# A two-layer trunk on one core: pacing of the modulation's row tiles beside the output projection, and another buffer pool for two filter tables

## The chip, the core and the metric

The kernel runs on one core of a Trainium2 chip. The metric is the device time of one execution in microseconds. Five engines take part: TensorE (PE) for matmuls, VectorE (DVE), ScalarE (ACT), GpSimd (POOL, nearly unused here) and SyncE (SP), whose queue issues nearly all loads. Each engine takes its instructions in one fixed order and waits at the first one that is not ready.

## The reference

A trunk of two layers over 256 tokens of width 2048, with 256 context tokens beside them. Each sub-layer is an RMS norm, modulated by shift, scale and gate vectors that are linear in the conditioning vector, then a mixer, then a gated residual.

```python
def _rms(x, g):
    xf = x.astype(jnp.float32)
    y = xf * lax.rsqrt(jnp.mean(xf * xf, axis=-1, keepdims=True) + EPS)
    return (y * g.astype(jnp.float32)).astype(x.dtype)
```

Layer 0 mixes with attention, layer 1 with an order-2 Hyena: projections, short convolutions, and long convolutions with filters that a small sine network makes from positions and that a decay table multiplies. Both layers end with a ConvGLU channel mixer of width 5632. The modulation has six vectors (parts 0 to 5) a layer: part (l, j) is the product of the conditioning vector with a 2048 x 2048 block of a weight matrix, plus a bias.

## The kernel before

All matmuls are in fp32 by parts: each operand is split into a high and a low part, and three products are summed (`products`, L343; `mm3`, L347 to L349). Weights come in blocks of 512 KB by SP (`wload`, L328) into a ring of six buffers ("raw"). `wsplit` makes the high part on ACT (L334) and the low part on DVE (L335), into rings of three each ("whi", "wlo").

The modulation's first two parts of layer 0 are made at the start on PE (`ada_block`, L924, its result copied by ACT into `adast`), from 512 KB loads that borrow the rings raw, whi, wlo and "araw" (six buffers, NAR). The other ten parts are made row tile by row tile on DVE: the class `Ada` has 32 row tiles for a part; `one()` issues the load of one tile into "araw" (L476) and, four tiles behind (LAG), multiplies and sums one tile in a single DVE instruction (L486, called a row sum below). L490 and L491 close a part. `drive(gen, rate, ada_rate)` runs a stage and, at each of its yields, adds `ada_rate` to a credit, of which each whole one pays for one `one()`. `need((l, j))` makes at once what a part still lacks. The flag `calm[0]` sets the rate to nothing:

```python
            ada_bg.step(0.0 if calm[0] else ada_rate if not isinstance(ada_rate, tuple) else ada_rate[0] if up else ada_rate[1])
```

`proj_out`, the output projection of every sub-layer, sets it for each of its steps, the last one true:

```python
                    calm[0] = final and half == 1 and i == n - 1
```

Only `proj_out` and the up projection of the channel mixer set it, so the Hyena's projections and convolutions (HY_ADA) run with what layer 0's channel mixer left. The Hyena's own output projection runs with HO_ADA:

```python
    drive(proj_out(hw_out, OUT_PASSES, h2split, adaV[:, 1, 2], xs, accs), HO_RATE, HO_ADA)
    need((1, 3), (1, 4))
```

Behind it stands the norm of layer 1's channel mixer: sums of squares on PE (L382), a reciprocal root by Newton steps of a few small DVE instructions (L384, L364 to L374, L390), and a broadcast on PE (L391). The channel mixer's first matmuls wait for that.

At the start `filters(DCS[0], True)` makes the spectra of the first two of four column blocks of the Hyena filters. For each block it loads the network's last weights (`w3`, L629, two halves of 256 KB) and the decay table (`dec`, L630, 512 KB), splits w3 on ACT and DVE (`w3s`, L358, L359), multiplies on PE (L347 to L349) and scales by the decay table (`hf`, L590). The start also takes the squares and norms of x and of the context (L662, L666, L671). Pool "q4" has 24 buffers of 512 KB, in which most tiles of the start and of the later stages live.

Of the kernel before, what the change touches and what calls it, by code (L numbers as in the profile page):

```python
# [12 lines left out]
F32 = mybir.dt.float32  # L13
# [6 lines left out]
P = 128  # L20
# [162 lines left out]
START_RATE = 2.0, 1.4  # L183
Q_RATE = 6.5
O_RATE = 5.2
KV_ADA, Q_ADA, O_ADA, HY_ADA, HO_ADA = 1.9, 0.7, 0.8, 0.2, 0.2
F0_ADA, F1_ADA = (0.7, 0.6), (0.4, 0.2)
EV_RATE, FLY, LAG = 1.0, 8, 4
DCS = (0, 1), (2,), (3,)
# [6 lines left out]
def trunk_kernel(ctx, tc, out, xT, cT, cols, rows, f_w0, f_w12, f_w3, ada_w, ada_t, w_in, w_out, hw_in, hw_out,  # L196
# [3 lines left out]
    NQ4, NS2, NRAW, NW, NAR = 24, 11, 6, 3, 6  # L200

    pool = ctx.enter_context(tc.tile_pool(name="pool", bufs=1))
# [4 lines left out]
    def nm(s):  # L207
        uid[0] += 1
        return f"{s}{uid[0]}"

    def q4(shape, dt=F32, name="q"):
        return pool.tile(shape, dt, tag="q4", bufs=NQ4, name=nm(name))

    def s2(shape, dt=F32, name="s"):
        return pool.tile(shape, dt, tag="s2", bufs=NS2, name=nm(name))
# [130 lines left out]
    def mm3(o, lh, ll, rh, rl, first, last, **kw):  # L346
        PE.matmul(o, lh, rh, start=first, stop=False, **kw)  # L347
        PE.matmul(o, lh, rl, start=False, stop=False, **kw)  # L348
        PE.matmul(o, ll, rh, start=False, stop=last, **kw)  # L349
# [7 lines left out]
    def split(hi, lo, src):  # L357
        A.copy(hi, src)  # L358
        V.tensor_tensor(lo, src, hi, op=ALU.subtract)  # L359
# [157 lines left out]
    def split_const(off, n, name, out=None):  # L517
        hi, lo = out or (q4([P, n], F32R, name + x) for x in "hl")
        for h in range(n // 512):
            t = s2([P, 512], F32, "fgt")  # L520
            c = slice(512 * h, 512 * h + 512)
            SP.dma_start(t, k_fg[:, off + 512 * h: off + 512 * h + 512])
            split(hi[:, c], lo[:, c], t)
        return hi, lo
# [40 lines left out]
    def filters(dcs, spare=False):  # L565

        if not dcs:
            return
        fhl = q4([P, 1024], F32R, "fm")
        split_const(0, 512, "f", (fhl[:, 0:512], fhl[:, 512:1024]))  # L570
        fh, fl = (fhl[:, i * 512:(i + 1) * 512].rearrange("p (t f) -> p t f", t=2) for i in range(2))
        w3v = f_w3.rearrange("w (o d c) -> w o d c", o=2, d=2)

        late = []

        def finish():
            for dst, sums in late:
                V.reciprocal(dst, sums)
            late.clear()

        def samples(o, dc, w3, dec, hl):
            nn = []
            for tt in range(2):
                ab = []
                for i, (sh, sl_) in enumerate(layers):
                    p = ftag[0]()
                    t = slice(tt * P, (tt + 1) * P)
                    mm3(p, sh[:, t], sl_[:, t], w3[0][:, o], w3[1][:, o], True, True)
                    h = s2([P, 512], F32, "hf")
                    V.tensor_tensor(h, p, dec[:, tt], op=ALU.mult)  # L590
                    split(hl[2 * i][:, tt], hl[2 * i + 1][:, tt], h)
                    A.activation(h, h, AF.Abs)
                    ab.append(h)
                    finish()
                    yield

                V.tensor_tensor(ab[0], ab[0], ab[1], op=ALU.max)
                nn.append(ab[0])
            V.tensor_tensor(nn[0], nn[0], nn[1], op=ALU.add)
            pn = ftag[0]()  # L600
            for c in range(4):
                PE.matmul(pn[:, c:c + 1], nn[0][:, c * P:(c + 1) * P], ones[:, 0:1], start=True, stop=True)
            late.append((invn[:, o, dc * 4:dc * 4 + 4], pn[:, 0:4]))

        def spectra(o, dc, hl):
            for half in range(2):
                so = q4([P, 2, 512], F32, "spo")
                xh, xl = hl[2 * half], hl[2 * half + 1]
                c = slice(half * P, (half + 1) * P)
                pe, po = ftag[0](), ftag[0]()  # L610
                mm3(pe, fh[:, 0, c], fl[:, 0, c], xh[:, 0], xl[:, 0], True, True)
                mm3(po, fh[:, 1, c], fl[:, 1, c], xh[:, 1], xl[:, 1], True, True)
                e = s2([P, 512], F32, "se")
                A.activation(e, pe, AF.Copy, scale=1.0 / (2 * T))
                V.scalar_tensor_tensor(out=so[:, 0], in0=po, scalar=1.0 / (2 * T), in1=e, op0=ALU.mult, op1=ALU.add)
                V.scalar_tensor_tensor(out=so[:, 1], in0=po, scalar=(half * 2 - 1) / (2 * T), in1=e, op0=ALU.mult,
                                       op1=ALU.subtract if half else ALU.add)
                yield
                A.dma_start(spec[o][dc][:, 2 * half:2 * half + 2], so)

        before = []
        for dc in dcs:
            if spare:
                w3 = pool.tile([P, 2, 512], F32, tag="araw", bufs=NAR, name=nm("w3"))
                dec = pool.tile([P, 2, 512], F32, tag="araw", bufs=NAR, name=nm("dec"))
            else:
                w3, dec = (q4([P, 2, 512], F32, "w3") for _ in range(2))
            for d in range(2):
                SP.dma_start(w3[d * HW:(d + 1) * HW], w3v[:, :, d, dc * 512:(dc + 1) * 512])  # L629
            SP.dma_start(dec, k_decay[:, :, dc * 512:(dc + 1) * 512])  # L630
            w3s = [q4([P, 2, 512], F32R, "w3s") for _ in range(2)]
            split(*w3s, w3)
            yield
            for o in range(2):
                hl = [q4([P, 2, 512], F32R, "fhl") for _ in range(4)]
                yield from samples(o, dc, w3s, dec, hl)
                if spare and before:
                    yield from spectra(*before.pop())
                before.append((o, dc, hl))
        if not spare:  # L640
            fill_rate[0] = 0.0
        finish()
        for b in before:
            yield from spectra(*b)
# [292 lines left out]

    bg.add(filter_net(), "filters")
    bg.add(filters(DCS[0], True), "filters")
    norm_bg = Bg()  # L940
    xg, cg = [], []
# [200 lines left out]
    def fill(dcs, at, rate):  # L1142

        def hook(*now):
            ftag[0] = HI4 if now[0] == 0 else LO4
            if dcs and now == at:
                fill_bg.add(filters(dcs), "fill")
                fill_bg.one()
                fill_rate[0] = rate
        return hook  # L1150
# [201 lines left out]
```

## Time and profile before

| what | value |
|---|---|
| median of 3 runs | 2630.94 us (2628.95 to 2631.34) |
| the profiled execution | 2630.88 us, its span 2629.1 us |
| granted PE clock, mean | 0.979 |
| PE busy | 2527.7 us (96%) |
| weight loads of PE busy | 2347.2 us (89%) |
| DVE busy | 1965.5 us (75%) |
| ACT busy | 1258.8 us (48%) |
| row sums L486 on DVE | 320, together 387.6 us |

Times of places are microseconds from the span's start. PE is close to always busy, so time is to be had or lost where PE waits: in the first 180 us, and at the seams between sub-layers.

### The profile page before, as it was taken

The page shows a single profiled execution, that of the slowest core. Times are in us where ns is not written, and L with a number is a line of the kernel's source. Part 1 is how long each engine was busy: PE and PEld are TensorE (multiplying, and loading weights), DVE is VectorE, ACT ScalarE, POOL GpSimd, SP SyncE. Part 2 cuts the span into 40 slices and gives each one's busy share as a digit, 9 for nine tenths or more (in the row PEclk, how much of TensorE's full clock was granted, in tenths as well). Part 3 has the DMA queues.
Part 4 walks back from the last instruction along what each step waited for, and adds up shares of the span by engine and source line. Part 5 has one row for each costly group of instructions (what it writes and reads, how often), then busy time and mean ns, then how long its engine had stood idle before and what let it go on. Part 6 is the DMA issues. An engine that isn't in the chain of part 4 may idle for free.

```text
span 2629.1 us, 48048 instructions
## 1 busy us (share of the span) xinstructions
PE 2527.7 (96%) x19502; PEld 2347.2 (89%) x19502; DVE 1965.5 (75%) x3071; ACT 1258.8 (48%) x1801; POOL 0.7 (0%) x6
## 2 busy tenths in 40 slices
PE   5889999999799999999999999999799999999999
PEld 2558886678799999999998999998799999999999
DVE  6637858877888888888878788889776755556664
ACT  3352235664544444445545655554354444445543
POOL 0000000000000000000000000000000000000000
PEclk7899999999899999999999999999899999999999
DMA  7777876557599999998897565555678766666664
GB/s 276 274 307 248 273 254 216 156 173 252 174 331 322 331 327 330 329 328 309 288 343 261 175 194 174 182 178 200 232 256 268 255 193 194 196 194 193 193 208 138
DMA packets 176726, 639.19 MB, mean 243 GB/s; under 512 B 19735, under 2 KB 19832, under 8 KB 176504
## 3 DMA queue, kind: packets, MB, share of 16 engines
q1 hardware_dynamic: 174200, 627.74, 71.8%
q10 hardware_dynamic: 2304, 8.39, 0.8%
q8 instruction: 152, 2.49, 0.4%
q14 instruction: 70, 0.57, 0.1%
HBM read 623.47 MB, written 12.58 MB: 242 GB/s over the span
## 4 chain that ended last, share of the span: by engine, by line
PE 90%; DVE 6%; ACT 3%; DMA 1%; issue 1%; SPq 0%; ACTq 0%; DVEq 0%
PE ps_proj L343 23%; PE ps_hy L343 9%; PE ps_kv L343 7%; PE ps_q L343 3%; PE ps_ada L343 2%; PE ps_ada L924 1%; PE ps_attn L853 1%; PE ps_attn L814 1%; DVE wlo_proj L335 1%; DVE araw_ada L486 1%; ACT whi_proj L334 1%; PE ps_conv L347 1%; PE ps_conv L348 1%; PE ps_conv L349 0%; PE ps_attn L773 0%
## 5 line engine op out<-in xcount | busy, mean ns | idle before, releaser
L335 DVE TENSOR_TENSOR wlo_proj<-raw_proj,whi_proj 128x1024 fp32r<-128x1024 f32 x240 | 292.4, 1222 | 144.2 <-ACT whi_proj L334 143.0
L334 ACT CAST whi_proj<-raw_proj 128x1024 fp32r<-128x1024 f32 x240 | 251.9, 1054 | 292.1 <-PE ps_proj L343 260.8
L486 DVE SCALAR_TENSOR_TENSOR araw_ada<-araw_ada,slB 128x1024 f32<-128x1024 f32 x320 | 387.6, 1218 | 0.0
L343 PE MATMUL ps_proj<-ph,whi_proj 128*128 128x256 f32 x1408 | 192.6, 277 | 1.1 <-ACT ph L358 1.0
L343 PE MATMUL ps_proj<-pl,whi_proj 128*128 128x256 f32 x1408 | 191.7, 277 | 0.0
L343 PE MATMUL ps_proj<-ph,wlo_proj 128*128 128x256 f32 x1408 | 191.1, 276 | 0.0
L343 PEld LDWEIGHTS ps_proj<-ph,whi_proj 128*128 128x128 f32 x1408 | 174.5, 188 | 2.8 <-ACT ph L358 1.7
L343 PEld LDWEIGHTS ps_proj<-pl,whi_proj 128*128 128x128 f32 x1408 | 174.4, 188 | 0.4 <-DVE pl L359 0.3
L343 PEld LDWEIGHTS ps_proj<-ph,wlo_proj 128*128 128x128 f32 x1408 | 174.1, 188 | 0.0
L334 ACT CAST whi_hy<-raw_hy 128x1024 fp32r<-128x1024 f32 x96 | 101.3, 1056 | 106.4 <-PE ps_hy L343 77.5
L335 DVE TENSOR_TENSOR wlo_hy<-raw_hy,whi_hy 128x1024 fp32r<-128x1024 f32 x96 | 116.3, 1221 | 45.5 <-ACT whi_hy L334 45.5
L343 PE MATMUL ps_hy<-hhi,whi_hy 128*128 128x256 f32 x768 | 109.3, 283 | 1.1 <-ACT hhi L423 1.1
L343 PE MATMUL ps_hy<-hlo,whi_hy 128*128 128x256 f32 x768 | 106.9, 280 | 0.0
L343 PE MATMUL ps_hy<-hhi,wlo_hy 128*128 128x256 f32 x768 | 105.3, 280 | 0.0
L343 PEld LDWEIGHTS ps_hy<-hhi,whi_hy 128*128 128x128 f32 x768 | 99.7, 190 | 3.4 <-ACT hhi L423 1.4
L343 PEld LDWEIGHTS ps_hy<-hlo,whi_hy 128*128 128x128 f32 x768 | 97.9, 190 | 0.8
L343 PEld LDWEIGHTS ps_hy<-hhi,wlo_hy 128*128 128x128 f32 x768 | 96.7, 190 | 0.1
L334 ACT CAST whi_kv<-raw_kv 128x1024 fp32r<-128x1024 f32 x40 | 42.0, 1053 | 105.8 <-PE ps_kv L343 94.0
L335 DVE TENSOR_TENSOR wlo_kv<-raw_kv,whi_kv 128x1024 fp32r<-128x1024 f32 x40 | 48.8, 1223 | 48.7 <-ACT whi_kv L334 48.7
L343 PE MATMUL ps_kv<-whi_kv,hhi 128*128 128x512 f32 x256 | 65.8, 398 | 0.0
L343 PE MATMUL ps_kv<-whi_kv,hlo 128*128 128x512 f32 x256 | 63.8, 391 | 0.0
L343 PE MATMUL ps_kv<-wlo_kv,hhi 128*128 128x512 f32 x256 | 63.8, 391 | 0.0
(9834 smaller groups left out, 7614.7 us busy)
## 6 DMA issues: line engine op xcount, KB each, us to landing
araw_ada<-ada_t SPq DMA_DIRECT2D x320, 512.0 KB, 5.1
raw_proj<-wd SPq DMA_DIRECT2D x176, 512.0 KB, 4.4
raw_hy<-hw_in SPq DMA_DIRECT2D x96, 512.0 KB, 3.8
raw_ada<-ada_w SPq DMA_DIRECT2D x46, 512.0 KB, 9.6
raw_kv<-w_in SPq DMA_DIRECT2D x40, 512.0 KB, 4.7
raw_q<-w_in SPq DMA_DIRECT2D x32, 512.0 KB, 4.4
raw_proj<-w_out SPq DMA_DIRECT2D x32, 512.0 KB, 4.9
raw_proj<-hw_out SPq DMA_DIRECT2D x32, 512.0 KB, 4.5
```

The costliest lines, as they stand in the source:

```text
L334: A.copy(hi, raw)
L335: V.tensor_tensor(lo, raw, hi, op=ALU.subtract)
L343: PE.matmul(o, ll if p == 2 else lh, rl if p == 1 else rh, start=first and p == 0, stop=last and p == 2, skip_group_check=True)
L347: PE.matmul(o, lh, rh, start=first, stop=False, **kw)
L348: PE.matmul(o, lh, rl, start=False, stop=False, **kw)
L486: V.scalar_tensor_tensor(out=raw, in0=raw, scalar=1.0, in1=slB[:, h * 1024:(h + 1) * 1024], op0=ALU.mult, op1=ALU.mult, accum_out=acc[:, h ...
L814: PE.matmul(ss_[m], qT[64 * m:64 * m + 64, h % 4, q_], KTa[h // 2][64 * m:64 * m + 64, h % 2], start=True, stop=True)
L853: PE.matmul(o[:, 0:P], wT[:, kt * P:(kt + 1) * P], v, start=kt == 0, stop=kt == 3)
L924: PE.matmul(pv[32 * q:32 * q + 32], sl[:, 2 * i + q], raws[q // 2][:, q % 2], start=i == 0, stop=i == 6, tile_position=(0, 32 * q))
```

## The change

Two rates are raised, that of the Hyena's projections and convolutions and that of its output projection. The first filters' two tables come from "q4" in place of "araw".

```diff
-KV_ADA, Q_ADA, O_ADA, HY_ADA, HO_ADA = 1.9, 0.7, 0.8, 0.2, 0.2
+KV_ADA, Q_ADA, O_ADA, HY_ADA, HO_ADA = 1.9, 0.7, 0.8, 0.3, 0.4
...
         for dc in dcs:
-            if spare:
-                w3 = pool.tile([P, 2, 512], F32, tag="araw", bufs=NAR, name=nm("w3"))
-                dec = pool.tile([P, 2, 512], F32, tag="araw", bufs=NAR, name=nm("dec"))
-            else:
-                w3, dec = (q4([P, 2, 512], F32, "w3") for _ in range(2))
+            w3, dec = (q4([P, 2, 512], F32, "w3") for _ in range(2))
```

From there on line numbers of the changed kernel are four lower (L629 is L625). The engines' orders show what moves. On SP, in the startup, the first block's tables stood ahead of the modulation's loads; before:

```order
L651 DMA x_155<-xT 128x1024
L629 DMA w_185<-f_w 64x2x512 x2
L630 DMA dec_186<-k_decay 128x2x512
L328 DMA raw_ada_60_195<-ada_w 128x1024
L328 DMA raw_ada_61_197<-ada_w 128x1024
L328 DMA raw_ada_80_269<-ada_w 128x1024
L522 DMA fgt_181<-k_fg 128x512
L328 DMA raw_ada_81_271<-ada_w 128x1024
L328 DMA raw_ada_90_316<-ada_w 128x1024
```

and now (`w` is w3; the name w_186 at L626 is the decay table):

```order
L647 DMA x_155<-xT 128x1024
L328 DMA raw_ada_60_195<-ada_w 128x1024
L328 DMA raw_ada_61_197<-ada_w 128x1024
L328 DMA raw_ada_80_269<-ada_w 128x1024
L328 DMA raw_ada_81_271<-ada_w 128x1024
L328 DMA raw_ada_90_316<-ada_w 128x1024
L328 DMA raw_ada_91_318<-ada_w 128x1024
L522 DMA fgt_181<-k_fg 128x512
L328 DMA raw_ada_111_398<-ada_w 128x1024
L328 DMA raw_ada_112_400<-ada_w 128x1024
L625 DMA w_185<-f_w 64x2x512 x2
L626 DMA w_186<-k_decay 128x2x512
```

They went from the place behind the loads of x to the place behind eight modulation loads and fgt. The second block's tables, also on SP, before:

```order
L651 DMA x_314<-cT 128x1024
L328 DMA raw_ada_132_493<-ada_w 128x1024
L629 DMA w_500<-f_w 64x2x512 x2
L630 DMA dec_501<-k_decay 128x2x512
L328 DMA raw_ada_143_523<-ada_w 128x1024
L328 DMA raw_ada_144_525<-ada_w 128x1024
L328 DMA raw_ada_149_550<-ada_w 128x1024
L328 DMA raw_ada_150_552<-ada_w 128x1024
```

and now:

```order
L328 DMA raw_ada_183_674<-ada_w 128x1024
L328 DMA raw_ada_189_701<-ada_w 128x1024
L328 DMA raw_ada_196_730<-ada_w 128x1024
L328 DMA raw_kv_203_758<-w_in 128x1024
L328 DMA raw_kv_206_788<-ada_w 128x1024
L625 DMA w_500<-f_w 64x2x512 x2
L626 DMA w_501<-k_decay 128x2x512
L328 DMA raw_kv_216_825<-ada_w 128x1024
```

They went from ahead of the fifteen weight loads that follow there in the old order up to raw_kv_206 to behind them: also behind raw_kv_206, which goes into the buffer of raw_kv_203 (the first key and value block) and waits until DVE has split that one.

On DVE, at the seam between the output projection and layer 1's channel mixer, the norm's Newton steps before (t is the step's small tile):

```order
L384 TENSOR_SCALAR t_20589<-ps_proj_3333_20578 128x2
L486 SCALAR_TENSOR_TENSOR araw_ada_20071,asum_14043<-araw_ada_20071,slB_86 128x1024
L364 TENSOR_SCALAR t_20592<-t_20589 128x2
L486 SCALAR_TENSOR_TENSOR araw_ada_20232,asum_14043<-araw_ada_20232,slB_86 128x1024
L365 TENSOR_SCALAR t_20591<-t_20592 128x2
L486 SCALAR_TENSOR_TENSOR araw_ada_20541,asum_14043<-araw_ada_20541,slB_86 128x1024
L367 TENSOR_TENSOR t_20592<-t_20591 128x2
L486 SCALAR_TENSOR_TENSOR araw_ada_20544,asum_14043<-araw_ada_20544,slB_86 128x1024
L368 SCALAR_TENSOR_TENSOR t_20592<-t_20592,t_20589 128x2
L486 SCALAR_TENSOR_TENSOR araw_ada_20547,asum_14043<-araw_ada_20547,slB_86 128x1024
L369 SCALAR_TENSOR_TENSOR t_20591<-t_20592,t_20591 128x2
L486 SCALAR_TENSOR_TENSOR araw_ada_20550,asum_14043<-araw_ada_20550,slB_86 128x1024
```

This goes on in pairs up to L373, with nine row sums in all, and then two low parts (L335) stand among L374, L490 and L390. Now:

```order
L384 TENSOR_SCALAR t_20589<-ps_proj_3333_20578 128x2
L486 SCALAR_TENSOR_TENSOR araw_ada_20293,asum_14043<-araw_ada_20293,slB_86 128x1024
L364 TENSOR_SCALAR t_20592<-t_20589 128x2
L486 SCALAR_TENSOR_TENSOR araw_ada_20372,asum_14043<-araw_ada_20372,slB_86 128x1024
L365 TENSOR_SCALAR t_20591<-t_20592 128x2
L486 SCALAR_TENSOR_TENSOR araw_ada_20559,asum_14043<-araw_ada_20559,slB_86 128x1024
L367 TENSOR_TENSOR t_20592<-t_20591 128x2
L335 TENSOR_TENSOR wlo_ffn1.0_3351_20665<-raw_ffn1.0_3349_20662,whi_ffn1.0_3350_20664 128x1024
L368 SCALAR_TENSOR_TENSOR t_20592<-t_20592,t_20589 128x2
L490 TENSOR_TENSOR asum_14043<-asum_14043 128x16
L335 TENSOR_TENSOR wlo_ffn1.0_3354_20695<-raw_ffn1.0_3352_20692,whi_ffn1.0_3353_20694 128x1024
L369 SCALAR_TENSOR_TENSOR t_20591<-t_20592,t_20591 128x2
```

Behind these rows come L491, L511 and the other Newton steps up to L390, with no more work of DVE that is not small. Three row sums and the same two low parts are left between L384 and L390. The six others stand earlier: DVE's order has 5 row sums within the output projection (ahead of the last residual sums) before, and 11 now. The DVE order of all stages from the keys and values up to the end of the Hyena's convolutions holds the same instructions in the same places.

## Rows read from the trace of the kernel before

**Rows 1.** The page's span, its chain by engine, one of its costliest groups.

```profile
span 2629.1 us, 48048 instructions
...
PE 90%; DVE 6%; ACT 3%; DMA 1%; issue 1%; SPq 0%; ACTq 0%; DVEq 0%
...
L486 DVE SCALAR_TENSOR_TENSOR araw_ada<-araw_ada,slB 128x1024 f32<-128x1024 f32 x320 | 387.6, 1218 | 0.0
```

**Rows 2.** Stretches of the span, tile araw_ada alone: VectorE busy us, clock, DMA.

```profile
1450.00:1775.00 325.00, 0.04 (x1) 0.99 0.58 179
...
1885.00:1895.00 10.00, 10.00 (x17) 0.50 0.89 306
```

**Rows 3.** Chain that ended last, 1860 to 1910: start us, us, what.

```profile
1884.37 0.16 DVE t L384
1884.53 1.14 DVE araw_ada L486 x2
...
1894.26 1.14 DVE araw_ada L486 x2
...
1896.77 1.14 DVE wlo_ffn1.0_3354_20695 L335
1897.90 0.21 DVE s L390
```

**Rows 4.** PE's timeline at the same place.

```profile
1898.16 1.22 PE L391 MATMUL ps_proj<-s,ones 128*128 128x128 f32 x4 [13.82 <-DVE s L390]
```

**Rows 5.** VectorE's timeline, an undisturbed norm chain in the startup.

```profile
62.19 0.16 DVE L384 TENSOR_SCALAR t<-ps_nc 128x2 f32<-128x2 f32 x1 [3.67 <-PE ps_nc L382]
...
64.37 0.48 DVE L390 TENSOR_SCALAR s<-ident,t 128x128 f32<-128x128 f32 x2
```

**Rows 6.** Output projection: busy us of PE, PEld, DVE, ACT, POOL; clock, DMA.

```profile
1800.00:1830.00 30.00, 27.77 (x197) 24.25 (x196) 29.56 (x61) 12.44 (x19) 0.00 (x0) 1.00 0.32 104
1830.00:1860.00 30.00, 29.76 (x250) 29.20 (x250) 21.06 (x28) 10.73 (x11) 0.00 (x0) 1.00 0.71 231
```

**Rows 7.** SyncE's waits, 0 to 205: in total, times, longest, us.

```profile
SPq L328 <- PE ps_ada L924: 36.6, 20, 9.0
SPq L328 <- DVE hf L590: 30.5, 2, 21.3
```

**Rows 8.** SyncE's timeline, 0 to 205: loads as they are issued.

```profile
4.62 1.34 SPq L629 DMA_DIRECT2D w<-f_w  x2
...
11.64 8.38 SPq L328 DMA_DIRECT2D raw_ada<-ada_w  x8
...
27.38 1.82 SPq L629 DMA_DIRECT2D w<-f_w  x2
...
66.07 5.35 SPq L328 DMA_DIRECT2D raw_ada<-ada_w  x4
...
79.88 0.33 SPq L328 DMA_DIRECT2D raw_kv<-ada_w  x1
```

**Rows 9.** Loads issued at 4.6 to 5.2: KB each, us to landing.

```profile
w<-f_w SPq DMA_DIRECT2D x1, 256.0 KB, 8.1
```

**Rows 10.** The same for loads issued at 15 to 17.2.

```profile
raw_ada<-ada_w SPq DMA_DIRECT2D x2, 512.0 KB, 9.6
```

**Rows 11.** The same for a load issued at 79.8 to 80.3.

```profile
raw_kv<-ada_w SPq DMA_DIRECT2D x1, 512.0 KB, 3.9
```

**Rows 12.** Chain that ended last, startup.

```profile
20.22 1.05 ACT w3s L358
...
26.15 0.70 DVE hf L590
...
66.79 5.15 PE ps_ada L924 x30
...
82.23 0.80 PE ps_filters L348
...
90.49 3.64 PE ps_ada L924 x32
```

## The prediction

> **What bounds the kernel now.** I read the page first: the chain that ended last is 90% PE, and DVE 6% [rows 1]. So the whole is bound by matmuls, and an edit off PE is worth only what it changes where PE waits. The profiled execution took 2630.88 us, with 2629.1 us of span [rows 1]; it stands at the median of the runs shown (2630.94), so the sum below is made against it and needs no correction. A change of 0.2% (5.3 us) is about what a measurement of this kernel can tell from none.
>
> Then I asked for the two places at which the orders differ. The first is the seam behind the Hyena's output projection. PE has nothing to do for 13.82 us before its broadcast at 1898.16, and waits for DVE's L390 [rows 4]. The chain there is DVE alone: a Newton step, a row sum, a Newton step, a row sum, from 1884.37 to 1897.90 [rows 3]. In the ten microseconds from 1885 DVE is busy on nothing else but row sums for practically all of it [rows 2]. The reader is to see that these are not filling a gap but are the gap: the same Newton chain without guests took from 62.19 to 64.37, that is 2.18 us for eleven steps, 0.2 us each [rows 5].
>
> The second place is the startup. There SP's loads wait for buffers: 36.6 us in all for matmuls of the modulation, and 30.5 us for `hf`, 21.3 us of it in one piece [rows 7]. That piece is a modulation load waiting for the decay table's "araw" buffer; the four loads behind it go from 66.07 on [rows 8]. The chain of the startup goes from the cast of w3 at 20.22 over `hf` at 26.15 and the two norms to the modulation's matmuls at 66.79, then over the second block's w3 (PE at 82.23) to the next modulation matmuls at 90.49 [rows 12].
>
> **The Hyena's rate costs and brings nothing.** Its steps run while `calm[0]` is still true from the last step of layer 0's channel mixer, so that rate is multiplied away. The trace bears it out: from 1450 to 1775 row sums take 0.04 us in 325 us, the one record being a tail [rows 2]; and DVE's order up to the end of the convolutions is the same. Term: 0. Were it to act, 0.1 a yield could only add row sums there, and there is no sign of one.
>
> **The output projection's rate, taken from the seam.** Nine row sums become three between L384 and L390; the two low parts (1.14 us and a little each [rows 3]) stay. One row sum is 1.218 us [rows 1]. Five pieces of about 1.22 make 6.1; of the eleven Newton steps some seven are no longer hidden behind a big piece, at 0.2 us each 1.4. Together 7.5 to 7.6 instead of 13.53 (1897.90 less 1884.37): −5.9 us. PE waits for this and nothing else there, so all of it counts at this place. Bounds: six row sums at full price are 7.3, less the 1.4 of steps that come into the open, so hardly more than −6; and if the loads that the three remaining ones need were late, each could give a microsecond or two back.
>
> **The same, given back earlier.** The six row sums now run inside the output projection. 7.3 us of DVE work go there, and the question is only whether PE waits for DVE. From 1800 to 1830 it does: DVE is busy 29.56 of 30 us and PE 27.77 [rows 6]. From 1830 to 1860 it doesn't: PE 29.76, DVE 21.06, with nine microseconds free [rows 6]. By the new order about two more fall into the first stretch (2.4 us at most), two or three into the second (free, or a few tenths each where one stands ahead of a low part), and one or two into the last pass, where residual sums and low parts follow each other closely (up to 1.2 each). I take +2.5; the ends are +0.5 (all find gaps) and +6 (PE waits for nearly all). Seam and projection together: −3.4, from −5.5 to 0.
>
> **The first block's tables come later.** They were issued at 4.62 and landed 8.1 us later, at about 13 [rows 8, 9], long before the cast at 20.22 [rows 12]. Now eight modulation loads and fgt are ahead. The eight loads from 11.64 took 8.38 us to issue, 1.05 each, and such loads landed 9.6 us after issue [rows 8, 10]. The tables' new place was reached at about 16.9 before, but 1 MB less (the tables themselves) is now ahead, so I put their issue at 14 to 15 and the landing at 24 to 24.5. The cast then comes about 4 us late. From cast to `hf` took 5.93 us before, with modulation matmuls between [rows 12]; these will have been done in the meantime, so I take about 1.8 off. Term: +2.3 (1 to 4). Hidden cover is gone here: what hid this load was being first.
>
> **The second block's tables come later.** They were issued from 27.38 [rows 8], 50 us ahead of use. Now they stand right behind raw_kv_206, which waits for DVE's split of the first key and value block and was issued at 79.88 [rows 8]. With the +2.3 from above and 0.33 us for that issue, w3 goes at about 82.5. Its two halves take a little; a load issued alone at this place landed in 3.9 us [rows 11], so w3 is there at about 86.8. The cast (1.05 [rows 12]) and the subtraction (as a low part, 1.2) follow: the first matmul with the low part at about 89.1, against 82.23 [rows 12], +6.9. What stood in the chain behind it runs to 90.49 with some half microsecond to spare, which leaves +6.4 for both tables together, so this term is +4.1 on top of +2.3 (bounds 2 and 6: the lower if the key and value block comes sooner, the upper if five loads that go shortly before it are still in the queues). From 100 us on loads and the matmuls that free their buffers follow each other in turn, and I find no slack that would take it up.
>
> **The wait that goes.** The modulation loads no longer wait for the decay table's buffer. But the load after those four goes into a buffer that the modulation's matmuls free, and these start at 66.79 whatever SP does [rows 12]; SP's other 36.6 us are for just that [rows 7]. So the 21.3 us become a wait of the same length for PE, and what is gained is about one load's share of the 5.35 us in which four went [rows 8], 1.3 at most. I take −0.9 (0 to −5.35, if all four loads counted). The Trainium skill, Perfetto Trace Analysis, Optimization Strategy, says that a gap that keeps coming back can mean too few buffers for the next tile; by it the buffer would be the cause and the term −5.35, the sum 2628.5. The rows on PE speak against it: the gap is there for want of a finished matmul too.
>
> **Sum.** Startup +2.3 +4.1 −0.9 = +5.5; seam −5.9 +2.5 = −3.4; together +2.1 on 2630.88: **2633.0 us**.
>
> **The rivals.**
> Faster: the four loads count in full, −5.35, and the second tables' lateness stays at its lower end, +2, since with those four early the modulation's copy is ready sooner. Startup 2.3 + 2 − 5.35 = −1.0, seam −5.0 (given back little): 2624.9. For it: the longest of SP's waits is gone. Against: the chain goes over PE and w3, not over these loads. It decides if modulation matmuls start at or before 90.49. (By the skill's rule on buffers named above it would go this way.) Chance 0.14.
> Slower: the second w3 alone. Its load competes with the loads issued just before it, and lands like those of the crowded queue, 9.6 us [rows 10], not 3.9: 5.7 later, +8 to +12 for the startup. It decides from +8.7 on, when that first low-part matmul starts later than 91; at +10.5 it gives 2630.88 + 10.5 − 3.4 = 2638.0. For it: five loads go within a few microseconds ahead of it. Against: SP itself paces them by PE. Chance 0.19.
> The seam gives nothing: PE waits in the projection for all that DVE now does there, +5.9: 2630.88 + 5.5 = 2636.4. For it is the stretch 1800 to 1830; against it the next one [rows 6]. Chance 0.10.
>
> **How the numbers follow.** The forecast's own case has 0.57, nearly all within 0.2% (2625.6 to 2636.1). Faster by more than that: 0.11, all from the first rival, whose other 0.03 lie within. Slower: 0.15 from the late w3, 0.04 from the seam without gain, 0.03 from the likeliest with both terms at their upper ends, 0.22. Within: 0.67. The likeliest case alone spans 2629 to 2637; the range goes to 2625 and 2640 to hold most of the rivals.
>
> **What would show it.** In the changed kernel's profile: no row sums between 1450 and 1775, as before; PE's wait before the broadcast L391 at the seam down from 13.82 to about 8, with three row sums in the chain; PE's busy time from 1800 to 1830 down by one or two microseconds; the first `hf` pair near 28.5 instead of 26.15; a cast of the second w3 near 87 that waits for its load; modulation matmuls that began at 90.49 near 96.5. It would be wrong if the first tables landed before 20, if the second w3's cast were not what PE waits for at 80 to 90, if the startup's delay were taken up before 180, or if PE's waits in the output projection grew by as much as the seam shrank.

## The result, and the profile after

The changed kernel takes 2649.97 us in the median of 4 runs (2644.78 to 2653.27); before, 2631.14 in as many. The ratio is 1.0067, with an interval of 1.0043 to 1.0090: 17.6 us longer by the ratio, from 11.3 to 23.7. The forecast was 2633.0 with a range up to 2640, so it was wrong, in size and in what it held likeliest. (The means differ by 17.5 us, the medians by 18.8; the ratios here lie near those of the means.) The profiled execution took 2647.93 us, its span is 2646.1, 17.0 more than before [rows 1].

Where these 17.0 us arise is seen by laying the same casts of weights (ACT, L334) of both traces side by side, 760 of them in the same order. The first key and value block is 3.8 us late, blocks of the keys and values from 211 us on 13.3, and so it stays to the end of the Hyena's convolutions. Within the output projection it grows to 17.0, behind the seam it is 10.7, at 1949 12.1; from 1990 to 2122 it grows by 5.1 to 17.2 and stays there. So: startup +13.3, output projection +3.7, seam −6.3, layer 1's channel mixer +6.5.

**Startup.** SP's timeline of the changed kernel, loads as they are issued:

```profile
13.71 1.81 SPq L625 DMA_DIRECT2D w<-f_w  x2
16.27 0.56 SPq L626 DMA_DIRECT2D w<-k_decay  x1
...
83.68 0.33 SPq L328 DMA_DIRECT2D raw_kv<-ada_w  x1
84.06 1.19 SPq L625 DMA_DIRECT2D w<-f_w  x2
85.30 0.60 SPq L626 DMA_DIRECT2D w<-k_decay  x1
```

ACT's two casts of w3 at the start, in the changed kernel:

```profile
24.77 1.04 ACT L358 CAST w3s<-w 128x1024 fp32r<-128x1024 f32 x1 [2.26 <-DMA w<-f_w]
...
92.22 1.04 ACT L358 CAST w3s<-w 128x1024 fp32r<-128x1024 f32 x1 [9.82 <-DMA w<-f_w]
```

and PE behind the second one:

```profile
93.31 1.22 PE L347 MATMUL ps_filters<-w3s,fah 128*128 128x512 f32 x2 [12.15 <-ACT w3s L358]
94.57 0.80 PE L348 MATMUL ps_filters<-w3s,fah 128*128 128x512 f32 x1
...
101.81 2.78 PE L920 MATMUL ps_ada<-raw_ada,sl 128*32 128x512 f32 x23 [1.02 <-ACT adast L924]
```

The first cast is at 24.77 where it was at 20.22, the second at 92.22; the first matmul with the low part is at 94.57 in place of 82.23, the modulation matmuls at 101.81 in place of 90.49 [rows 12]. The bracket names the cause: PE had nothing for 12.15 us and waited for that cast, which waited for w3's load. The transfers from 85.0 to 92.3, that is from 0.9 us after that load's issue to the cast (q1 is the queue of SP's loads, q10 of ACT's stores; the last figure is the share of the 16 DMA engines' time):

```profile
DMA packets 784, 1.96 MB, mean 269 GB/s; under 512 B 70, under 2 KB 70, under 8 KB 784
...
q1 hardware_dynamic: 640, 1.44, 78.1%
q10 hardware_dynamic: 144, 0.52, 20.2%
...
spec<-spo ACTq DMA_DIRECT2D x1, 512.0 KB, 6.2
w<-k_decay SPq DMA_DIRECT2D x1, 512.0 KB
```

and the same two queues in the kernel before, from 79.9 to 83.8, while the load of [rows 11] was under way:

```profile
q1 hardware_dynamic: 144, 0.52, 44.9%
q10 hardware_dynamic: 97, 0.39, 26.5%
```

The load of w3 was issued at 84.06, 0.4 us behind 512 KB of modulation weights (raw_kv_206), and the decay table followed it. Its cast could start 8.2 us after its issue, where the load of [rows 11], the first in its queue, landed in 3.9. A store from ACT ran beside that one too, so the store is not what differs. What differs is SP's own queue: 1.44 MB in 7.3 us, with the DMA engines busy for 98% of the time, against 0.52 MB in 3.9 us and 71%. The Trainium skill (DMA: Bandwidth & Descriptors, Issuing engines are not separate DMA queues) has loads and stores of different engines interleave on the same 16 DMA engines; the trace agrees, with 0.52 MB on q10 among 1.44 MB on q1.

SP's waits from 0 to 205, in total, times and longest, in the changed kernel:

```profile
SPq L328 <- PE ps_ada L920: 73.8, 19, 27.3
SPq L328 <- DVE wlo_kv L335: 24.9, 6, 8.0
```

The wait for the decay table's buffer [rows 7] is gone, and the one for the modulation's matmuls has grown from 36.6 to 73.8 us, by more than what went.

**Output projection and seam.** PE's broadcast at the seam, changed kernel:

```profile
1909.21 1.22 PE L391 MATMUL ps_proj<-s,ones 128*128 128x128 f32 x4 [7.70 <-DVE s L390]
```

PE's waits from the output projection to the first matmuls of the channel mixer, changed kernel, and then the row of before that answers to the second:

```profile
PE ps_proj L391 <- DVE s L390: 7.7, 1, 7.7
PE ps_proj L343 <- DVE wlo_proj L335: 4.5, 6, 1.1
```

```profile
PE ps_proj L343 <- DVE wlo_proj L335: 1.3, 2, 1.1
```

The wait at the seam fell from 13.82 [rows 4] to 7.70 us, and the waits for low parts grew by 3.2. Two stretches of the output projection (columns as in [rows 6], and these two answer to them):

```profile
1813.00:1843.00 30.00, 27.46 (x198) 24.47 (x197) 29.66 (x61) 12.36 (x19) 0.00 (x0) 1.00 0.36 112
1843.00:1873.00 30.00, 28.50 (x236) 27.73 (x237) 23.23 (x31) 10.80 (x11) 0.00 (x0) 1.00 0.76 265
```

In the first PE is busy 27.46 us, hardly less than the 27.77 of before; in the second, where DVE had nine microseconds free, PE fell from 29.76 to 28.50. That fall is no new loss. It comes from waits that moved over the edges of the stretches, as PE's single waits for low parts show; before:

```profile
1829.79 1.21 PE L343 MATMUL ps_proj<-h2h,wlo_proj 128*128 128x256 f32 x8 [1.06 <-DVE wlo_proj L335]
...
1857.89 0.50 PE L343 MATMUL ps_proj<-h2h,wlo_proj 128*128 128x256 f32 x2 [0.23 <-DVE wlo_proj L335]
```

and in the changed kernel:

```profile
1825.87 0.50 PE L343 MATMUL ps_proj<-h2h,wlo_proj 128*128 128x256 f32 x2 [0.57 <-DVE wlo_proj L335]
...
1836.32 1.19 PE L343 MATMUL ps_proj<-h2h,wlo_proj 128*128 128x256 f32 x8 [1.14 <-DVE wlo_proj L335]
...
1846.68 1.21 PE L343 MATMUL ps_proj<-h2h,wlo_proj 128*128 128x256 f32 x8 [0.82 <-DVE wlo_proj L335]
...
1866.21 0.50 PE L343 MATMUL ps_proj<-h2h,wlo_proj 128*128 128x256 f32 x2 [0.25 <-DVE wlo_proj L335]
...
1879.40 0.51 PE L343 MATMUL ps_proj<-h2h,wlo_proj 128*128 128x256 f32 x2 [0.86 <-DVE wlo_proj L335]
...
1886.78 0.50 PE L343 MATMUL ps_proj<-h2h,wlo_proj 128*128 128x256 f32 x2 [0.86 <-DVE wlo_proj L335]
```

By the order of the matmuls, the wait of 1.06 us at the end of the old first stretch corresponds to the 0.82 us at 1846.68, now in the second, and 0.23 to 0.25. Up to 1846.68 the waits are 1.5 us longer, in the stretch with DVE's nine free microseconds nothing is added, and in the last pass, where DVE now has a row sum ahead of a low part twice (at 1876.64 and 1884.03), 1.7 us are.

**The Hyena.** Row sums (tile araw_ada) on VectorE from the end of layer 0 to the output projection:

```profile
1463.00:1788.00 325.00, 1.22 (x2) 0.99 0.58 178
```

One sum (each leaves two records), the first of the output projection's, in 325 us: the rate does nothing.

**Layer 1's channel mixer.** The same matmuls run slower there, without a gap and with the clock granted in full. A stretch of before, and one of the changed kernel (PE busy us and count first, granted clock third from the end):

```profile
2040.00:2080.00 40.00, 40.00 (x355) 40.00 (x355) 27.20 (x36) 17.50 (x21) 0.00 (x0) 1.00 0.82 273
```

```profile
2040.00:2080.00 40.00, 40.00 (x342) 40.00 (x341) 28.30 (x38) 18.18 (x23) 0.00 (x0) 1.00 0.80 258
```

342 matmuls in 40 us where there were 355; by the trace, each takes 281 ns and starts 117.8 ns after the one before it, where 276 and 113.3 ns are usual. It does so in 43 us behind the seam and in 136 us from 2003 on, and that is the +6.5.

### The profile page after: what moved, and what is told of

Read it like the earlier page. It is cut to its first block, busy times and chain, and to the rows that moved or that the text cites. A ratio compares the mean times of both kernels' runs of the same rounds, so it can differ in the third digit from the quotient of the medians.

```text
span 2646.1 us, 48046 instructions
## 1 busy us (share of the span) xinstructions
PE 2534.4 (96%) x19502; PEld 2354.8 (89%) x19502; DVE 1965.2 (74%) x3071; ACT 1258.0 (48%) x1801; POOL 0.7 (0%) x6
## 5 line engine op out<-in xcount | busy, mean ns | idle before, releaser
L335 DVE TENSOR_TENSOR wlo_proj<-raw_proj,whi_proj 128x1024 fp32r<-128x1024 f32 x240 | 292.4, 1222 | 140.0 <-ACT whi_proj L334 138.5
L334 ACT CAST whi_proj<-raw_proj 128x1024 fp32r<-128x1024 f32 x240 | 251.6, 1054 | 289.7 <-PE ps_proj L343 250.2
L334 ACT CAST whi_hy<-raw_hy 128x1024 fp32r<-128x1024 f32 x96 | 101.3, 1056 | 106.7 <-PE ps_hy L343 77.6
L335 DVE TENSOR_TENSOR wlo_hy<-raw_hy,whi_hy 128x1024 fp32r<-128x1024 f32 x96 | 116.5, 1223 | 45.5 <-ACT whi_hy L334 45.5
L334 ACT CAST whi_kv<-raw_kv 128x1024 fp32r<-128x1024 f32 x40 | 42.0, 1052 | 113.8 <-PE ps_kv L343 95.0
L335 DVE TENSOR_TENSOR wlo_kv<-raw_kv,whi_kv 128x1024 fp32r<-128x1024 f32 x40 | 48.9, 1224 | 46.5 <-ACT whi_kv L334 46.4
```

The lines of the kernel that those rows point to most:

```text
L334: A.copy(hi, raw)
L335: V.tensor_tensor(lo, raw, hi, op=ALU.subtract)
```

## The experiments

Times are against the kernel before, run on the same chip; 1% is 26.3 us.

**The rates alone.** Tables in araw:

```diff
-KV_ADA, Q_ADA, O_ADA, HY_ADA, HO_ADA = 1.9, 0.7, 0.8, 0.2, 0.2
+KV_ADA, Q_ADA, O_ADA, HY_ADA, HO_ADA = 1.9, 0.7, 0.8, 0.3, 0.4
```

> The two rates of the change alone, the tables left in araw. Theory 1 (the tables' late loads make the startup's 13.3 us, and the slower pace of the matmuls in layer 1's channel mixer is no part of what the rates do): startup as before, the first low-part matmul of the second tables at about 82 and the modulation matmuls at about 90.5; PE's wait before L391 down from 13.8 to about 7.7 us, PE's waits for the low parts of the output projection's weights up from 1.3 to about 4.5 us, so the whole is 2 to 3 us shorter than before, about 2629. Theory 2 (the slower pace, 281 ns a matmul in place of 276, comes with the rates, through the way in which PE comes out of the seam): the same seam, but about 6 us are lost again until 2120, so some 4 us longer than before, about 2635.

Measured: 0.9998 (0.9987 to 1.0009), that is −0.5 us, from −3.4 to +2.4. PE's waits from the output projection to the channel mixer:

```profile
PE ps_proj L391 <- DVE s L390: 7.7, 1, 7.7
PE ps_proj L343 <- DVE wlo_proj L335: 4.4, 6, 1.1
```

The seam's 6.1 us are got, 3.1 us are given back in waits for low parts. Of the slower pace 43 us came behind the seam, none from 2003 on. So the rates neither pay nor cost what these runs can measure (theory 1's 2 to 3 us lie within the interval), and their order alone did not bring the long spell of slower matmuls in this execution.

**The tables alone.** The second hunk of the change, rates of before.

> The tables alone in q4, both rates of before. Theory 1: the whole startup loss and nothing else: about +13, 2644, with the wait for the second w3's cast at PE of about 12 us, and no difference from the Hyena to the end beyond the shift. Theory 2: the same +13, since the slower pace belongs to the rates. Theory 3 (the slower pace comes with any shift of the later stages against each other): +19, 2650, with matmuls of 281 ns in layer 1's channel mixer. A loss under 5 us would speak against the startup as the place.

Measured: 1.0057 (1.0039 to 1.0075), +15.0 us (10.3 to 19.7), with the same wait for the cast as the first of PE's waits:

```profile
PE ps_filters L347 <- ACT w3s L358: 12.1, 1, 12.1
```

Matmuls in layer 1's channel mixer had the usual pace here. Within the intervals this is the whole loss. In this profile 11.1 us of it stand behind the startup, by the casts; another 3.2 arise near 445, where the granted clock (third from the end) fell from 1.00 to 0.50 for seven microseconds:

```profile
440.00:455.00 15.00, 15.00 (x56) 9.75 (x57) 10.36 (x22) 8.17 (x19) 0.00 (x0) 0.77 0.46 157
```

In the kernel before it stayed at 1.00 there, though PE was idle for the same 1.35 us in the five ahead of it. Nothing on record ties this to the tables.

**One block's tables at a time.** The first block's alone, and the second's alone:

```diff
-            if spare:
+            if spare and dc != 0:
...
-            if spare:
+            if spare and dc != 1:
```

> Only the first column block's tables come from q4, the second's from araw as before; rates of before. SP then issues the second block's tables after seven more loads, still some 50 us ahead of use. Theory 1, in which the second block's late load is two thirds of the loss: the first hf pair some 3 to 4 us late as in the changed kernel, PE's 12.2 us wait for the cast of the second w3 gone, and the startup 3 to 5 us longer than before: about 2635. Rival: the loss comes from the first tables, or from what the later norm chain does to the clock: 10 us or more, 2641.

> Only the second column block's tables come from q4, the first's from araw as before; rates of before. SP issues the second tables right behind raw_kv_206 again. Theory 1 (the second w3's landing is what PE waits for, and the first tables' delay adds to it): PE's wait for the cast of the second w3 about 12 us as in the changed kernel, the modulation matmuls of 90.5 at about 98, the whole 7 to 11 us longer than before, about 2640; with the first block alone (+4 by its runs) this makes up the +15 of both. Rival (what hurts is both together, since the first block's delay pushes the issue of the second): less than 4 us.

Measured: the first block 1.0015 (1.0001 to 1.0029), +3.9 us (0.3 to 7.6); the second 1.0040 (1.0024 to 1.0055), +10.5 (6.3 to 14.5). They add up to 14.4, against 15.0 for both; behind the startup the casts of the two profiles are 2.1 and 9.1 us late, together 11.2, against 11.1 for both. With the first alone the second cast has no wait:

```profile
25.30 1.04 ACT L358 CAST w3s<-w 128x1024 fp32r<-128x1024 f32 x1 [2.76 <-DMA w<-f_w]
...
81.91 1.04 ACT L358 CAST w3s<-w 128x1024 fp32r<-128x1024 f32 x1
```

and with the second alone the first cast is where it was, and PE waits 12.0 us for the second:

```profile
20.17 1.04 ACT L358 CAST w3s<-w 128x1024 fp32r<-128x1024 f32 x1
...
88.01 1.04 ACT L358 CAST w3s<-w 128x1024 fp32r<-128x1024 f32 x1 [10.00 <-DMA w<-f_w]
```

```profile
PE ps_filters L347 <- ACT w3s L358: 12.0, 1, 12.0
```

So most of the loss comes with the second block's tables, and it needs no help from the first. This run also shows the slower pace of matmuls, in the same stretch of the channel mixer as the changed kernel, with the order of before there:

```profile
2040.00:2080.00 40.00, 40.00 (x342) 40.00 (x341) 28.31 (x38) 17.79 (x23) 0.00 (x0) 1.00 0.79 256
```

**The decay tables alone.** dec from q4, w3 from araw:

```diff
-                dec = pool.tile([P, 2, 512], F32, tag="araw", bufs=NAR, name=nm("dec"))
+                dec = q4([P, 2, 512], F32, "dec")
```

> Only the two decay tables come from q4, both w3 from araw as before; rates of before. SP issues w3 of both blocks at their old places, the first decay table after seven modulation loads and the second behind raw_kv_206, and the modulation loads wait no more for the decay table's buffer. Theory 1 (w3's lateness is the loss, since its cast is first in the chain; the wait that goes brings a microsecond at most): no cast of w3 that PE waits for, the time within 3 us of before, 2629 to 2633. Rival A (the decay table late is just as bad, as the first product hf needs it): 2638 to 2642. Rival B (the removed wait of 21.3 us pays once w3 is early): 2625.

Measured: 1.0013 (1.0001 to 1.0026), +3.4 us (0.3 to 6.8): just beyond theory 1's three microseconds, and far from a gain. PE waits for no cast, but 2.9 us for the product with the table that is now late:

```profile
PE ps_filters L347 <- DVE hf L590: 2.9, 1, 2.9
```

The second decay table, now the only table behind raw_kv_206 (issued at 81.59), took 7.2 us to land, raw_kv_206 itself 3.7:

```profile
raw_kv<-ada_w SPq DMA_DIRECT2D x1, 512.0 KB, 3.7
dec<-k_decay SPq DMA_DIRECT2D x1, 512.0 KB, 7.2
```

Its profile shows the slower pace in layer 0's channel mixer, which no part of the edit touches:

```profile
840.00:880.00 40.00, 40.00 (x342) 40.00 (x341) 32.07 (x46) 17.98 (x22) 0.00 (x0) 1.00 0.90 321
```

**The Hyena's rate alone.**

```diff
-KV_ADA, Q_ADA, O_ADA, HY_ADA, HO_ADA = 1.9, 0.7, 0.8, 0.2, 0.2
+KV_ADA, Q_ADA, O_ADA, HY_ADA, HO_ADA = 1.9, 0.7, 0.8, 0.3, 0.2
```

> The Hyena's rate alone, 0.3 in place of 0.2, all else as before. Theory 1: nothing, 2631, since the rate is multiplied away; no row sum between 1450 and 1775. Rival (it acts): nine or ten row sums among the Hyena's projections, time changed by more than the interval. It is also a second look at the order of before: if the slower pace of matmuls (281 ns) in layer 1's channel mixer is a matter of chance, it can show here without any change of the order.

Measured: 1.0000 (0.9990 to 1.0011), and not one row sum:

```profile
1450.00:1775.00 325.00, 0.00 (x0) 0.99 0.58 178
```

Its startup, in the order of before, is 2.4 us later at 211 us than that of the first profile. That much a single profile's startup scatters (−1.4 and +2.4 were the ends among the runs with this order), so differences of 2 us there are read from the timed runs.

**The tables early, in q4.** A function `tables(dc)` holds the allocation and the loads; the first block's call stands behind the loads of x, the second's at the first block's start; rates of before:

```diff
+            w3, dec = early.pop(0) if spare else tables(dc)
+            if spare and dc == dcs[0]:
+                early.append(tables(dcs[1]))
...
+    early = [tables(DCS[0][0])]
```

> The tables in q4 as in the change, but written earlier in the program, so that SP issues the first block's right behind the loads of x (its old place) and the second block's seven loads later, at about 14; rates of before, 0.2 and 0.2. The modulation loads wait no more for the decay table's buffer. Theory 1 (what costs is the tables' place in SP's order, not their pool, and the wait that goes was one for PE too): PE's 12 us wait for the cast of the second w3 gone, SP's 21.3 us wait now put down to the modulation's matmuls, time within 2 us of before: 2629 to 2632. Rival A (the freed wait pays): 5 us shorter, 2625. Rival B (the pool itself costs, through other tiles that then wait for q4 buffers): still some 10 us longer, 2640.

Measured: 1.0008 (0.9999 to 1.0017), +2.1 us, from −0.3 to +4.5. SP's waits:

```profile
SPq L328 <- PE ps_ada L925: 59.2, 19, 21.2
```

The pool is not what costs: the rival's 10 us lie outside the interval. And the 21.3 us that SP waited for `hf` [rows 7] are now a wait of 21.2 us for the modulation's matmuls: the loads were early enough without it.

**The Hyena's rate in force.** Ahead of its projections, tables in araw; first with the rates of before, then with 0.3 and 0.4:

```diff
+    calm[0] = False
     for dc in range(4):
         for part in range(3):
             drive(hy_proj(dc, part), HY_RATE, HY_ADA)
```

> The flag is set false ahead of the Hyena's projections, so that its rate of 0.2 acts; tables in araw, the output projection's rate 0.2 as before. The row sums that stood between the seam's Newton steps are then made among the Hyena's projections, where DVE is busy 265 of 319 us and PE waits for it 0.2 us in all. Theory 1 (row sums cost only where PE waits for DVE): none between L384 and L390 but the two low parts, PE's wait before L391 down from 13.8 to about 5, no new waits of PE among the Hyena's projections, the whole 7 to 9 us shorter, about 2623. Rival (row sums in the Hyena cost PE as much as in the output projection, 0.5 us each or more): 19 of them give back 9 us or more, 2630 or later.

> The flag set false as in the run before, and the change's rates 0.3 and 0.4; tables in araw. About ten more row sums go into the Hyena and six more into its output projection than in the run before, taken from layer 1's channel mixer, where PE doesn't wait for DVE. Theory 1: the seam as in the run before (about 5 us of wait), but the output projection's PE waits for low parts are up by 3 to 4 us as with the changed rate alone, so 3 to 4 us longer than the run before, 2626 to 2627. Rival (where the row sums stand matters little): the same as the run before, 2623.

Measured: 0.9949 (0.9931 to 0.9967), 13.4 us shorter than before (8.7 to 18.2), with 0.2; and 0.9960 (0.9946 to 0.9974), 10.5 us shorter (6.8 to 14.2), with the rates of the change. Row sums and PE's waits in the first of the two:

```profile
1454.00:1775.00 321.00, 24.57 (x40) 1.00 0.65 211
```

```profile
PE ps_proj L391 <- DVE s L390: 2.6, 1, 2.6
...
PE ps_proj L343 <- DVE wlo_proj L335: 0.5, 1, 0.5
```

Twenty row sums stand in the Hyena, where PE has no wait worth a row, and the seam's wait is 2.6 us, less than the 5 expected, since the low parts had gone ahead too. With the higher rates PE waits for low parts 3.6 us, as theory 1 had it, but the intervals of the two times overlap. The first of the two has the lowest time of the study, and it does what the change's first rate names. Its profile is 9.3 us ahead of that of before, not 13.4. Its Hyena projections take 2.3 us longer, with matmuls at a slower pace (see layer 1's channel mixer above) and no wait. The run of the rates alone shows the same with no row sum there, and the next run shows only 0.2 us with the same twenty, so the row sums are not shown to cost anything.

> The kernel of the run before this one and, with it, the flag set false ahead of the Hyena's projections (rate 0.2 there and 0.2 in the output projection). Theory 1: the two parts are apart in place and add up, so the time is that of the kernel in which the Hyena's rate acts, 12 to 14 us below before, about 2619 to 2621. Rival (freed wait pays): 2615.

Both edits together: 0.9977 (0.9965 to 0.9988), −6.0 us. The sum of the parts would be −11.3. The profiled executions differ less than the timed runs: from the seam on this one is 9.1 us ahead of that of before, and the one with the Hyena's rate alone 9.3. The timed runs of the two were made on different chips; whether their difference is more than scatter is open.

**A higher rate in the output projection.** 0.6, tables in araw.

> The output projection's rate at 0.6, tables in araw, the Hyena's rate as before (without effect). By DVE's order no row sum is left between the seam's Newton steps; all of them stand in the output projection. Theory 1 (each row sum moved there gives back about half a microsecond, as 3.2 us for six at 0.4): PE's wait before L391 down from 13.8 to about 2.6, PE's waits for low parts in the output projection up from 1.3 to 7 us or more, net 4 to 5 us shorter than before, 2626. Rival (DVE is full there, and each moved row sum beyond the first six is paid in full): no change from before, 2631, with PE's waits for low parts up to 10 us or more.

Measured: 0.9990 (0.9981 to 0.9999), −2.6 us, between the two. PE's waits:

```profile
PE ps_proj L343 <- DVE wlo_proj L335: 5.4, 7, 1.1
PE ps_proj L391 <- DVE s L390: 2.6, 1, 2.6
```

The seam's wait is 11.2 us shorter. Against before, PE's matmuls of the output projection start 0.9 us late and end 8.7 late, so 7.8 us are given back there, 4.1 of them in waits for low parts.

## Why the prediction was wrong, step by step

**The Hyena's rate: 0.** Right, shown by the run of it alone and by the one in which it acts.

**The seam: −5.9.** Right: −6.1 in both profiles with the changed rates.

**Given back in the output projection: +2.5.** Mis-sized: +3.7 in the changed kernel, 3.2 in the run of the rates alone, within the bounds (0.5 to 6). By place the step was right: the first stretch cost 1.5 us more (forecast 2.4 at most), the second nothing, and the last pass 1.7, two row sums at 0.86 each (forecast up to 1.2). Only the sum was taken too low. Seam and projection are −2.6 by the profile in place of −3.4, and −0.5 (−3.4 to +2.4) by the runs.

**The first block's tables: +2.3.** Within its bounds: the second `hf` product came at 29.24 instead of 26.15, +3.1, and by the run of it alone +3.9 (0.3 to 7.6).

**The second block's tables: +4.1 on top.** This is the term that failed most. Its place in SP's order, the wait for raw_kv_206 and the chain behind the cast were right. The step that failed is "a load issued alone at this place landed in 3.9 us". The load that took 3.9 us was raw_kv_206 itself, the first in its queue; w3 stands behind it, with the decay table behind w3. The cast came at 92.22, 5.4 us later than the forecast 86.8. Of that, 1.6 is the issue (84.06, forecast 82.5) and 3.9 the landing: 8.2 us from issue to cast, where the forecast allowed 4.3. Measured, the term is +10.5 by the run of it alone (6.3 to 14.5), 9 to 11 by the casts. This is the mechanism of the rival "the second w3 alone", which had 0.19 and 2638.0; the time went beyond it too. How much of the landing is the crowd and how much the load's own form was not separated. Of the loads of w3 and the decay tables whose landing the traces have, 66 in all, none landed in less than 4.9 us, and the decay table took 7.2 at this place without w3. The 3.9 us of another kind of load were too little for that reason too.

**The wait that goes: −0.9.** Nothing was got. With the tables early and the wait gone, the kernel takes +2.1 us (−0.3 to +4.5), and SP's 21.2 us are a wait for PE, as the step said. The Trainium skill (Perfetto Trace Analysis, Optimization Strategy) says that the same gap, repeating on the engine that should be saturated, can mean too few buffers. The gap here was one wait of SP, not a repeating one of PE, so this case hardly tests the rule; what the run shows is that freeing the buffer gained no time.

**What no step had.** The slower matmuls of layer 1's channel mixer, +6.5 us in the profiled execution. They also came with the order of before there (the second block's tables alone), and in layer 0's channel mixer (the decay tables alone), and in the rates alone only for the first 43 us. So no new order of that stage is needed for them, and they may be part of the scatter of executions (before ranged from 2626.8 to 2641.9 in 29 runs). But the long spell stands in three of the thirteen traces, and all three are of kernels whose second decay table comes late; the fourth such trace, the tables alone, has none. Whether late tables make it more frequent is not settled: the changed kernel's 4 runs lie 17.6 us above before, the tables alone 15.0, and the intervals overlap.

**Sum.** Measured in the profile: startup +13.3, projection +3.7, seam −6.3, slower matmuls +6.5: +17.2, against 17.0 between the spans. By parts that were timed: tables +15.0, rates −0.5, together +14.5 against +17.6 (11.3 to 23.7). In the profile the startup is 7.8 us above its forecast of +5.5 (2.0 of it arise between 101.81 and 211, and no run shows why), the slower matmuls add 6.5, the projection 1.2. Without the slower matmuls this execution would stand at about 2641.4 (an estimate, 2647.93 less 6.5), just beyond the range. Part of the miss is thus a thing whose cause is open; that the tables cost more than the forecast said is shown by their own runs (+15.0, at least 10.3, for +5.5).

## What to carry to other kernels

When a change moves a load in a queue, its landing time is to be taken from what stands ahead of it and beside it in the new order, not from the nearest load of the old one: here one load that came 3.9 us later than assumed held up the cast, and PE with it. A queue's wait for a buffer costs nothing if a second wait, for something else, would hold the same loads just as long: when the buffer was free, SP waited 21.2 us for PE in place of 21.3 for the buffer. And before a rate is tuned, see in the trace that it acts: the flag in front of it hid some 13 us by the runs and 9 by the profile, while raising both rates without it brought 0.5 (from 3.4 to a loss of 2.4).

## What was not expected of the hardware

Matmuls of 128x256 that follow one another without a gap have two paces at a granted clock of 1.00: 113.3 ns from start to start, or 117.8 (355 or 342 in 40 us). In the channel mixers the slower one came in spells, one of some 43 us right behind the seam's idle time, once the granted clock was back at 1.00, and a second of 136 us some 44 us later; in other executions only the first, or none. In the Hyena the two paces are mixed in every trace. No wait, no gap and no lower granted clock goes with it in the trace. The two spells together cost 6 to 7 us of an execution. What starts and ends them is open.
